# The last two output chunks of the second layer computed as seven block products

## The chip, the cores and the metric

The kernel runs on one core of a Trainium2 chip. The metric is the device time in microseconds of one execution; the median of the runs is compared.

## The reference, cut to what matters

The network is two layers of a hybrid encoder trunk (256 tokens, width 2048). Everything that the change touches is the last line of a layer:

```
merged = jnp.zeros_like(x)
for n, (y, z) in enumerate(((y_a, a_z), (y_b, b_z), (y_c, c_z), (y_m, m_z))):
    branch = y.reshape(B, S, W).astype(dt) * jax.nn.silu(z)
    merged = merged + jax.nn.sigmoid(gate_all[:, :, n]) * (branch @ w_branch[n])
return x + merged @ w_out
```

`merged` is 256 x 2048 and `w_out` 2048 x 2048, both float32. The output of the second layer is the result of the kernel.

## The kernel before, in words

**Matrix products.** Weights stream from DRAM in slabs of 512 rows by 512 columns (1 MB, a tile `raw`, four buffers, loaded by the SP queue). A slab is cut in two halves of 256 rows. ACT rounds a half to a float32r tile `whi`, DVE takes the difference as `wlo` (`cut_piece`, both 128x1024); four buffers each. The activations are cut in the same way (`mg0h`, `mg0l` and so on), and three matmuls (high x high, high x low, low x high) stand for one float32 product. A half of a slab feeds 12 matmuls of 512 columns: two 128-row steps of the contraction, two blocks of 128 tokens, three terms.

**The stream.** `advance`, called after each half, runs waiting tasks (`pump`) and cuts the half that is four halves ahead (`split_weights`). `gemm_plan` writes down the slabs in the order of use; `plan` is that order, `cuts` says for each half whether it comes from a slab or from a chain of sums. All engines execute their instructions in the order in which this program issues them, so the order of calls in Python is the order on each queue.

**Products already in use.** Two places of each layer (group `c`, and the gate chunks 2 and 3 of each branch, `DUO`) compute two neighbouring 512-column chunks as a 2x2 block product with seven instead of eight block multiplications (`product`, `take`, `combined`). A block is 1024 rows by 512 columns of weights, against 128 tokens by 1024: 24 matmuls, four pieces of 256 rows with 6 matmuls each. The token side needs sums of the blocks of its matrix (`s1`, `s2`, `s3`, `r4`, made by `forms` on DVE and cut by ACT and DVE). The weight side needs running sums: four tiles `sum` are loaded by SP, and after each use the next block is added to them by an accumulating DMA from the POOL queue (`add_block`).

**The end of the second layer.** For each 512-column piece d of `merged`, the last branch's `bridge` adds into `acc[d]`, and the task `merged(d)` turns it: a DVE transpose inside 32x32 squares (`mgpi`), sixteen 32 KB DMA moves (`mgp`, taken in turns by POOL and SP, placed in the program by `tick`), a rest of some ticks, then the cut into `mg..h` and `mg..l`. The pieces come in the order 0, 3, 2, 1, and `w_out`'s rows are stored in that order. Then `w_out` is applied: chunks 0 and 1 side by side, chunk 2, chunk 3, each of four slabs, 16 slabs in all. `added(c)` loads the residual (`x1`, kept in DRAM) and adds it on DVE to the product in PSUM, one 128-token half after the other, and each half is stored by SP. In the last slab of chunk 3 the matmuls are sorted so that the first token half ends early.

Of the kernel before, what the change touches and what calls it, by code (L numbers as in the profile page):

```python
# [158 lines left out]
BETWEEN_PRODUCTS = (4, 3, 4, 4, 3, 2, 3)  # L159
MOVES, STEPS, BANKS, WARM = 5, 2, 2, 7  # L160
# [125 lines left out]
def gemm_plan(wmem, win, wbr, wout):  # L286
    p, cuts, starts = [], [], {}
# [24 lines left out]
    for l in range(L):  # L312
# [18 lines left out]
        pair(SIDE_ORDER, *((wout, (l * 4 + c) * DM * 512) for c in range(2)))  # L331
        for c in range(2, 4):
            add(wout, (l * 4 + c) * DM * 512, 512)
    return p, cuts, starts
# [9 lines left out]
def trunk(ctx: ExitStack, tc: tile.TileContext, x, xt, memt, ng, qkg, hg, lbl, win, wmem, wbr, wout,  # L344
# [40 lines left out]
    plan, cuts, starts = gemm_plan(wmem, win, wbr, wout)  # L385
# [31 lines left out]
    def split_weights():  # L417
        if stream.cut in starts:
            group = starts[stream.cut]
            chains[group] = [G([128, 2, 512], "sum") for h in range(4)]  # L420
            for h in range(4):
                add_block(group, STAGES[0], h)
        group, i, h = cuts[stream.cut] or (None, None, None)
        if group and i != RING:
            cut_piece(*half(512), chains[group][h])
            if i < 4:
                add_block(group, STAGES[i + 1], h)
            elif i == 4 and group[1] != "c":
# [12 lines left out]
        if group and group[1] == "c":  # L441
# [4 lines left out]
    def add_block(group, stage, h):  # L446
        adds, rows, d = stage
        to = chains[group][h].rearrange("p k n -> p (k n)")
        block = dram(win, columns(*group)[d] + (2 * rows + h // 2) * 512 * 512 + h % 2 * 1024, 2048, 1024)
        if adds:  # L450
# [732 lines left out]
    for l in range(L):  # L1183
# [44 lines left out]

        def forms(l=l):
# [3 lines left out]
            def total(out, sign, first, second):  # L1233
                for p in range(2):
                    at, a, b = (u[p] if isinstance(u, tuple) else blocks(u[:, 4 * p:4 * p + 4, :]) for u in (out, first, second))
                    (ve.tensor_add if sign > 0 else ve.tensor_sub)(at, a, b)
                    yield

            def parts(name, out):
                hi, lo = (spool.tile([128, 8, 128], F32R, tag="s", name=name + e) for e in "hl")  # L1240
                ac.copy(hi, out)
                yield
                ve.tensor_sub(lo, out, hi.bitcast(F32))
                yield
                return hi, lo

# [155 lines left out]
        def bridge(n, d, gt, l=l):  # L1402
# [12 lines left out]
            if n == BR_ORDER[-1]:  # L1415
                mg.append(stream.add(merged(d)))

# [25 lines left out]
        nx = []  # L1443
# [19 lines left out]
        wo = [(wout, (l * 4 + c) * DM * 512) for c in range(4)]  # L1463
        gemms(mg, wo[:2], 512, ["wo", "wo"], order=[(i, b, j) for i, b in SIDE_ORDER for j in range(2)], then=[added(0), added(1)])
        later = [added(c) for c in (2, 3)]
        for c in (2, 3):
            later[c - 2](gemm(mg, *wo[c], 512, "wo", tail=l == L - 1 and c == 3))
        if l + 1 < L:
            xh, rs = nx, stream.add(scale_of(nssq, list(nx), 1))
# [50 lines left out]
```

## Time and profile before

| | us |
|---|---|
| median of 3 runs (1810.14 to 1810.40) | 1810.35 |
| the profiled execution | 1809.55 |
| its span, first to last instruction | 1807.5 |
| around the span | 2.05 |

The profile is of one execution. In its rows PE is TensorE's matmuls, PEld its weight loads, DVE VectorE, ACT ScalarE, POOL GpSimd, SP the SyncE that issues DMAs; `SPq` marks the issue of a DMA on that queue. Busy times of engines overlap, and the row of matmuls shows the modelled length of each, which is longer than the distance from one to the next. Times in a timeline are from the start of the span.

### The profile page before, as it was taken

How to read it: one execution, taken by the hardware profiler on the slowest of the kernel's cores; microseconds unless marked ns; L12 is line 12 of the kernel's file. 1: busy time of each engine (PE TensorE's matmuls, PEld its weight loads, DVE VectorE, ACT ScalarE, POOL GpSimd, SP SyncE). 2: the span in 40 equal slices, each digit the busy share in tenths (PEclk: the TensorE clock that was granted, in tenths of full speed). 3: DMA queues.
4: the chain of work that ended last, by engine and by line, in shares of the span. 5: the costliest groups of instructions: out<-in, count | busy, mean ns of one | idle time of the engine just before them, and what ended most of it. 6: DMA issues, size and time to landing. Idle time of an engine off the chain costs nothing.

```text
span 1807.5 us, 24344 instructions
## 1 busy us (share of the span) xinstructions
PE 1801.9 (100%) x8836; PEld 1499.9 (83%) x8836; DVE 1345.9 (74%) x1458; ACT 1059.3 (59%) x1261; POOL 379.9 (21%) x573
## 2 busy tenths in 40 slices
PE   9999999999999999999999999999999999999999
PEld 8889888888888888888888988888888888888887
DVE  5677798786878777687666779878787877767764
ACT  5756565455667656554455656545666765656442
POOL 0022330033232111112032342003332211110200
PEclk9999999999999999999999999999999999999999
DMA  9769965779899999986694996568999989998773
GB/s 337 268 213 290 290 210 179 256 227 276 271 263 272 294 227 275 263 245 216 229 296 160 314 266 210 195 235 240 264 289 253 284 274 231 274 264 232 238 233 135
DMA packets 124936, 451.44 MB, mean 250 GB/s; under 512 B 23184, under 2 KB 44944, under 8 KB 92048
## 3 DMA queue, kind: packets, MB, share of 16 engines
q1 hardware_dynamic: 89840, 357.45, 56.7%
q0 software_dynamic: 34688, 92.18, 26.2%
q8 instruction: 69, 1.13, 0.3%
q14 instruction: 51, 0.42, 0.1%
q10 hardware_dynamic: 288, 0.26, 0.0%
HBM read 419.66 MB, written 6.29 MB: 236 GB/s over the span
## 4 chain that ended last, share of the span: by engine, by line
PE 99%; DMA 0%; DVE 0%; SPq 0%; ACT 0%; issue 0%
PE u L145 51%; PE px L145 21%; PE bw L145 10%; PE wo L145 10%; PE mv L145 2%; PE mk L145 2%; PE ixrp L145 0%; PE mov L145 0%; PE mlg L145 0%; PE bo L145 0%; PE co L145 0%; PE aov L145 0%; PE cl L145 0%; PE bs L145 0%; PE alg L145 0%; DMA raw<-in_wmem 0%
## 5 line engine op out<-in xcount | busy, mean ns | idle before, releaser
L127 DVE TENSOR_TENSOR wlo<-raw,whi 128x1024 fp32r<-128x1024 f32 (+3 forms) x556 | 655.3, 1187 | 341.0 <-ACT whi L127 335.1
L127 ACT CAST whi<-raw 128x1024 fp32r<-128x1024 f32 (+3 forms) x556 | 568.1, 1025 | 571.5 <-PE u L145 340.4
L127 DVE TENSOR_TENSOR wlo<-sum,whi 128x1024 fp32r<-128x1024 f32 x240 | 288.2, 1221 | 62.4 <-ACT whi L127 54.9
L127 ACT CAST whi<-sum 128x1024 fp32r<-128x1024 f32 x240 | 250.5, 1052 | 99.7 <-PE px L145 51.3
L127 POOL DMA_DIRECT2D sum<-in_win x152 | 137.4, 910 | 607.0 <-DVE wlo L127 556.2
L145 PE MATMUL u<-whi,x01h 128*128 128x512 f32 (+2 forms) x176 | 67.5, 383 | 0.0
L145 PE MATMUL u<-whi,x11h 128*128 128x512 f32 (+2 forms) x176 | 67.5, 383 | 0.0
L145 PE MATMUL u<-whi,x12h 128*128 128x512 f32 (+2 forms) x176 | 67.4, 383 | 0.0
L145 PE MATMUL u<-whi,x02h 128*128 128x512 f32 (+2 forms) x176 | 67.4, 383 | 0.0
L145 PE MATMUL u<-whi,x10h 128*128 128x512 f32 (+2 forms) x176 | 67.3, 383 | 0.0
L145 PE MATMUL u<-whi,x00h 128*128 128x512 f32 (+2 forms) x176 | 67.3, 383 | 0.0
L145 PE MATMUL u<-whi,x03h 128*128 128x512 f32 (+2 forms) x176 | 67.1, 381 | 0.0
L145 PE MATMUL u<-whi,x13h 128*128 128x512 f32 (+2 forms) x176 | 67.1, 381 | 0.0
L145 PE MATMUL u<-wlo,x11h 128*128 128x512 f32 (+2 forms) x176 | 67.0, 381 | 0.0
L145 PE MATMUL u<-wlo,x01h 128*128 128x512 f32 (+2 forms) x176 | 67.0, 381 | 0.0
L145 PE MATMUL u<-wlo,x12h 128*128 128x512 f32 (+2 forms) x176 | 67.0, 381 | 0.0
L145 PE MATMUL u<-wlo,x02h 128*128 128x512 f32 (+2 forms) x176 | 67.0, 381 | 0.0
L145 PE MATMUL u<-wlo,x10h 128*128 128x512 f32 (+2 forms) x176 | 67.0, 381 | 0.0
L145 PE MATMUL u<-wlo,x00h 128*128 128x512 f32 (+2 forms) x176 | 67.0, 381 | 0.0
L145 PE MATMUL u<-whi,x00l 128*128 128x512 f32 (+2 forms) x176 | 67.0, 381 | 0.0
L145 PE MATMUL u<-whi,x10l 128*128 128x512 f32 (+2 forms) x176 | 67.0, 381 | 0.0
L145 PE MATMUL u<-wlo,x03h 128*128 128x512 f32 (+2 forms) x176 | 67.0, 381 | 0.0
(496 smaller groups left out, 4488.7 us busy)
## 6 DMA issues: line engine op xcount, KB each, us to landing
raw<-in_win SPq DMA_DIRECT2D x180, 1024.0 KB, 6.5
sum<-in_win POOLq DMA_DIRECT2D x152, 512.0 KB, 8.5
sum<-in_win SPq DMA_DIRECT2D x80, 512.0 KB, 6.9
raw<-in_wbr SPq DMA_DIRECT2D x32, 1024.0 KB, 6.3
raw<-in_wout SPq DMA_DIRECT2D x32, 1024.0 KB, 5.6
raw<-in_wmem SPq DMA_DIRECT2D x12, 1024.0 KB, 6.0
raw<-in_win SPq DMA_DIRECT2D x8, 656.0 KB, 4.1
xc<-in_x SPq DMA_DIRECT2D x8, 512.0 KB, 7.1
```

The lines of the kernel that those rows point to most:

```text
L127: return call(*args, **kw)
L145: return self.engine.matmul(out, w, x, **kw)
```

## The change

Layer 1 keeps its output projection. In layer 2 the chunks 0 and 1 stay slabs of 512 rows, and the chunks 2 and 3 become seven block products, written in between by `LAST_ORDER` (pairs are chunk and slab, single numbers are products). There are two chains of sums: `sumy` (products 2, 3, 4, 6) and `sumx` (product 1); products 0 and 5 take raw slabs. `LAST_BEGIN` says how many cuts ahead a chain is loaded and added to. The token-side sums come from the turned `merged` pieces by a task `last_forms`; the last piece is turned by moves on POOL alone, and its first two task steps are made at once. The residual of chunk 0 and of chunk 3 is added by an accumulating DMA instead of DVE.

```
+LAST_ORDER = ((0, 0), (1, 0), (0, 1), (1, 1), 2, (0, 2), 1, (1, 2), 3, (0, 3), 4, 0, (1, 3), 5, 6)
+LAST_RAW, LAST_NEXT = {0: (1, 1), 5: (1, 0)}, {2: (True, 0, 1), 3: (True, 1, 1), 4: (True, 1, 0)}
+LAST_BEGIN = {2: ((AHEAD, "y", (False, 0, 0)),), 1: ((2 * AHEAD, "x", (False, 0, 1)), (AHEAD, "x", (True, 1, 1)))}
...
+    def last_product(l, i, part):
+        if i in LAST_RAW:
+            rows, d = LAST_RAW[i]
+            p.append((wout, (l * 4 + 2 + d) * DM * 512 + (2 * rows + part) * 512 * 512, 512))
+        if not part:
+            for ahead, chain, stage in LAST_BEGIN.get(i, ()):
+                begins[len(cuts) - ahead] = chain, stage
+        cuts.extend(("last", i, 2 * part + k) for k in range(2))
...
+        if stream.cut in begins:
+            chain, stage = begins[stream.cut]
+            if chain not in chains:
+                chains[chain] = [G([128, 2, 512], "sum" + chain) for h in range(4)]
+            for h in range(4):
+                last_block(chain, stage, h)
         group, i, h = cuts[stream.cut] or (None, None, None)
-        if group and i != RING:
+        if group == "last" and i not in LAST_RAW:
+            chain = "x" if i == 1 else "y"
+            cut_piece(*half(512), chains[chain][h])
+            if i in LAST_NEXT:
+                last_block(chain, LAST_NEXT[i], h)
+            return
...
+    def last_block(chain, stage, h):
+        adds, rows, d = stage
+        to = chains[chain][h].rearrange("p k n -> p (k n)")
+        block = dram(wout, ((L - 1) * 4 + 2 + d) * DM * 512 + (2 * rows + h // 2) * 512 * 512 + h % 2 * 1024, 2048, 1024)
         if adds:
             po.dma_start(to, block, accum_op=OP.add)
         else:
             sy.dma_start(to, block)
...
-        def merged(d):
-            u = yield from transposed(acc[d], "mgp", 3 if d == MERGED[-1] else 4)
-            return split(u, gen, "g", f"mg{d}")
+        def merged(d, l=l):
+            u = yield from transposed(acc[d], "mgp", *((3, (po,) if l + 1 == L else (po, sy)) if d == MERGED[-1] else (4,)))
+            if l + 1 < L:
+                return split(u, gen, "g", f"mg{d}")
+            last_rows[MERGED.index(d)] = u
+            return split(u, xtp, "xt", f"mg{d}")
+
+        def last_forms():
...
+            r4 = G([128, 8, 128], "r4")
+            yield from total(r4, -1, quarter(0, 0), quarter(0, 1))
+            last_made["s3"] = yield from parts("s3", r4)
+            while len(last_rows) < 4:
+                yield BLOCKED
+            s1, s2 = (G([128, 8, 128], name) for name in ("s1", "s2"))
+            yield from total(s1, -1, quarter(0, 1), quarter(2, 1))
+            last_made["s1"] = yield from parts("s1", s1)
+            yield from total(s2, -1, s1, quarter(0, 0))
+            last_made["s2"] = yield from parts("s2", s2)
+            yield from total(r4, 1, s2, quarter(2, 0))
+            last_made["r4"] = yield from parts("r4", r4)
...
             if n == BR_ORDER[-1]:
                 mg.append(stream.add(merged(d)))
+                if d == MERGED[-1] and l + 1 == L:
+                    mg[-1].step()
+                    mg[-1].step()
...
+    def second_column():
+        qs, us = got["qs"], got["us"]
+        ve.tensor_tensor(qs, qs, us[:, 0:1, :].to_broadcast([128, 2, 512]), op=OP.subtract)
+        yield
+        ve.tensor_tensor(us, qs, us[:, 1:2, :].to_broadcast([128, 2, 512]), op=OP.add)
+        po.dma_start(us, x1[:, :, 3 * 512:4 * 512], accum_op=OP.add)
+        yield
+        ve.tensor_sub(got["xc"][:, 1, :], got["xc"][:, 1, :], qs[:, 1, :])
+        got["less"] = True
+        yield from stream.rest(5)
+        sy.dma_start(out[:, :, 3 * 512:4 * 512], us)
...
+    def first_column(t, to):
+        xc = got["xc"]
+        ve.tensor_add(xc[:, t, :], to, xc[:, t, :])
+        sy.dma_start(out[:, t, 2 * 512:3 * 512], xc[:, t, :])
...
+    for at in LAST_ORDER:
+        if isinstance(at, tuple):
+            c, b = at
+            open_chunks[c] = gemms(mg, wo[c:c + 1], 512, ["wo"], order=[(0, b, j) for j in range(2)], tiles=open_chunks.get(c))
+            if b == 2 and c:
+                ends[c] = added(c)
+            elif b == 3:
+                (ends[c] if c else first_chunk)(open_chunks[c][0])
+        else:
+            last_take(at, 0)
+            last_take(at, 1)
```

**Place one: the last moves of `merged`.** On POOL, at the start of the output projection, the order of before and of the change; `mgp` are the moves of the turned pieces (8 for each of the first three, the rest for the last piece, d = 1), `sumx` and `sumy` adds of 512 KB, `xc` and `us` the residuals of chunks 0 and 3:

```order
 L127 DMA sum<-in_win 128x1024 x32
-L127 DMA mgp<-mgpi 32x2x128 x32
-L1514 UNCONDITIONAL_BRANCH
-L1514 ISA
+L127 DMA mgp<-mgpi 32x2x128 x28
+L127 DMA sumx<-in_wout 128x1024 x4
+L127 DMA mgp<-mgpi 32x2x128 x12
+L127 DMA sumy<-in_wout 128x1024 x12
+L127 DMA xc<-x_92 128x2x512
+L127 DMA us<-x_92 128x2x512
```

Four adds now stand between the fourth and the fifth of the sixteen moves of the last piece. On ACT, from the cut of the second piece (`mg3h`) on:

```order
 L127 CAST mg3h<-mgp 128x1024
-L127 CAST whi<-raw 128x1024 x5
+L127 CAST whi<-raw 128x1024 x3
+L127 CAST s3h<-r_14522 128x1024
+L127 CAST whi<-sumy 128x1024 x2
 L127 CAST mg2h<-mgp 128x1024
-L127 CAST whi<-raw 128x1024 x5
 L127 CAST mg1h<-mgp 128x1024
-L127 CAST whi<-raw 128x1024 x18
-L1514 UNCONDITIONAL_BRANCH
+L127 CAST whi<-sumy 128x1024 x2
```

The cut of the last piece, `mg1h`, had five slab halves between itself and `mg2h`; now it follows `mg2h` directly, ahead of the third and fourth piece of product 2 (the second pair of `whi<-sumy`).

**Place two: the token sum of product 0.** `r4` is the token side of product 0. On ACT and on DVE, from the cuts of product 4's last pieces on (`xc<-wo` copies chunk 0 out of PSUM):

```order
+L127 CAST whi<-sumy 128x1024 x2
+L127 COPY xc<-wo 128x512 x2
+L127 CAST whi<-raw 128x1024
+L127 CAST r4h<-r_14522 128x1024
+L127 CAST whi<-raw 128x1024 x7
```

```order
+L127 TENSOR_TENSOR wlo<-sumy,whi 128x1024
+L127 TENSOR_TENSOR wlo<-raw,whi 128x1024 x3
+L127 TENSOR_TENSOR r4l<-r_14522,r4h 128x1024
+L127 TENSOR_TENSOR wlo<-raw,whi 128x1024
+L127 TENSOR_TENSOR us<-us,px 128x512
```

The low part `r4l` stands behind the third of product 0's four weight pieces on DVE.

**Place three: the end.** On DVE, before and now (`xc<-px` is the first result column's add, `us` chunk 3):

```order
-L127 TENSOR_TENSOR xc<-wo,xc 128x512 x2
-L127 TENSOR_TENSOR wlo<-raw,whi 128x1024 x4
-L127 TENSOR_TENSOR xc<-wo,xc 128x512
-L127 TENSOR_TENSOR xc<-wo_14892,xc 128x512
-L1514 UNCONDITIONAL_BRANCH
+L127 TENSOR_TENSOR wlo<-sumy,whi 128x1024 x4
+L127 TENSOR_TENSOR xc<-px,xc 128x512
+L127 TENSOR_TENSOR us<-qs,us 128x1024
+L127 TENSOR_TENSOR xc<-xc,qs 128x512
+L127 TENSOR_TENSOR xc<-px,xc 128x512
```

The sum that finishes chunk 3 (`us<-qs,us`) now comes behind all four pieces of product 6 and behind the add that waits for product 5; POOL's add of the residual and SP's store of chunk 3 follow it.

## Rows read from the trace of the kernel before

**Rows 1.** The page, busy time by engine, and the chain that ended last by engine:

```profile
PE 1801.9 (100%) x8836; PEld 1499.9 (83%) x8836; DVE 1345.9 (74%) x1458; ACT 1059.3 (59%) x1261; POOL 379.9 (21%) x573
PE 99%; DMA 0%; DVE 0%; SPq 0%; ACT 0%; issue 0%
```

**Rows 2.** All waits of PE in the whole span: who waited for whom, us in total, times, longest:

```profile
PE heat L145 <- DVE warm L127: 1.1, 1, 1.1
PE mk L145 <- DVE wlo L127: 0.2, 1, 0.2
```

**Rows 3.** The chain that ended last, from 1716 us to the end: start, us, what:

```profile
1716.25 87.05 PE wo L145 x384
1803.30 0.02 issue
1803.32 0.69 DVE xc L127
```

**Rows 4.** The same chain in the stage of the gate products, one slab (`u`) and one product (`px`):

```profile
1541.95 5.44 PE u L145 x24
1547.39 5.44 PE px L145 x24
```

**Rows 5.** The timeline of DVE at the start of the output projection: start, us, engine, line, operation, count, idle time before it and who ended it:

```profile
1717.37 1.23 DVE L127 TENSOR_TENSOR wlo<-raw,whi 128x1024 fp32r<-128x1024 f32 x1 [1.49 <-ACT whi L127]
1718.51 1.22 DVE L127 TENSOR_TENSOR gate<-bw,gate 128x1024 f32<-128x1024 f32 x1
1719.77 1.22 DVE L127 TENSOR_TENSOR acc<-acc,gate 128x1024 f32<-128x1024 f32 x1
1720.91 1.22 DVE L127 TENSOR_TENSOR mg3l<-mgp,mg3h 128x1024 fp32r<-128x1024 f32 x1
...
1723.18 1.24 DVE L127 STREAM_TRANSPOSE mgpi<-acc 128x1024 f32<-128x1024 f32 x1
```

**Rows 6.** The timeline of ACT, the cut of the last piece between two halves of slabs, and a pair of copies out of PSUM:

```profile
1711.80 1.26 ACT L127 ACTIVATE gate<-u,rs1r 128x512 f32<-128x512 f32 x2
...
1743.48 1.05 ACT L127 CAST whi<-raw 128x1024 fp32r<-128x1024 f32 x1 [1.67 <-PE wo L145]
1744.44 1.05 ACT L127 CAST mg1h<-mgp 128x1024 fp32r<-128x1024 f32 x1
```

**Rows 7.** The timeline of POOL, the last piece's moves before the change, as the POOL queue issued them:

```profile
1724.71 1.58 POOL L127 DMA_DIRECT2D mgp<-mgpi  x3 [13.74 <-DVE mgpi L127]
1726.56 2.63 POOL L127 DMA_DIRECT2D mgp<-mgpi  x5 [0.27 <-issue]
```

**Rows 8.** The timeline of POOL in an earlier stage, four adds and then eight moves (`bnpt`) on the same queue:

```profile
1381.29 0.91 POOL L127 DMA_DIRECT2D sum<-in_win  x1 [5.71 <-DVE wlo L127]
1382.43 0.86 POOL L127 DMA_DIRECT2D sum<-in_win  x1 [0.23 <-issue]
1387.48 0.85 POOL L127 DMA_DIRECT2D sum<-in_win  x1 [4.19 <-DVE wlo L127]
1390.30 0.86 POOL L127 DMA_DIRECT2D sum<-in_win  x1 [1.97 <-DVE wlo L127]
1390.83 3.03 POOL L127 DMA_DIRECT2D bnpt<-bnpti  x5
1395.87 0.54 POOL L127 DMA_DIRECT2D bnpt<-bnpti  x1 [2.00 <-DMA sum<-in_win]
1398.20 0.53 POOL L127 DMA_DIRECT2D bnpt<-bnpti  x1 [1.79 <-DMA sum<-in_win]
1401.15 0.53 POOL L127 DMA_DIRECT2D bnpt<-bnpti  x1 [2.41 <-DMA sum<-in_win]
```

**Rows 9.** From issue to landing, the 28 adds of POOL from 1490 to 1700 us, then the 64 moves `mgp` of layer 2 (the row of POOL's 32 and the landing of all), then the 8 stores of the result: length of the issue min/median/max in ns, first and last start:

```profile
L127 POOL DMA_DIRECT2D sum<-in_win x28: 853/862/973, 1492.7 to 1641.9; - x28
DMA to landing us min/median/max: 5.9/8.6/10.8
...
L127 POOL DMA_DIRECT2D mgp<-mgpi x32: 533/533/587, 1685.9 to 1728.7; - x32
DMA to landing us min/median/max: 1.8/4.9/6.7
...
L1456 SPq DMA_DIRECT2D out<-xc x8: 332/338/344, 1757.3 to 1804.0; - x8
DMA to landing us min/median/max: 2.0/4.1/8.5
```

**Rows 10.** DMA from 1560 to 1640 us (80 us of the gate products): packets, MB and share of 16 engines by queue (q0 is POOL's, q1 SP's):

```profile
q0 software_dynamic: 1963, 7.18, 52.0%
q1 hardware_dynamic: 2259, 12.94, 43.7%
```

**Rows 11.** Stretches: length, busy time of PE, PEld, DVE, ACT, POOL (and instructions), granted clock, share of the 16 DMA engines, GB/s:

```profile
1738.00:1760.00 22.00, 22.00 (x99) 18.22 (x98) 12.14 (x11) 9.58 (x10) 0.00 (x0) 1.00 0.59 192
1760.00:1781.00 21.00, 21.00 (x94) 17.38 (x94) 10.84 (x10) 8.24 (x8) 0.00 (x0) 1.00 0.81 276
1781.00:1803.30 22.30, 22.29 (x99) 18.12 (x97) 8.17 (x9) 5.28 (x5) 0.00 (x0) 1.00 0.07 25
1560.00:1640.00 80.00, 80.00 (x354) 66.10 (x353) 58.04 (x50) 47.68 (x51) 12.13 (x14) 1.00 0.96 252
```

**Rows 12.** The timeline of SP, the first load of `w_out`, loads while the last piece is turned, and the last stores (four merged, the last at 1804.0):

```profile
1691.42 0.33 SPq L400 DMA_DIRECT2D raw<-in_wout  x1
...
1718.62 0.33 SPq L400 DMA_DIRECT2D raw<-in_wout  x1
...
1725.55 4.29 SPq L400 DMA_DIRECT2D raw<-in_wout  x2
...
1784.51 19.87 SPq L1456 DMA_DIRECT2D out<-xc  x4
```

**Rows 13.** The timeline of PE in the first microseconds of the span:

```profile
1.13 3.35 PE L145 MATMUL heat<-warm 128*128 128x128 f32 x14 [1.13 <-DVE warm L127]
...
5.92 0.41 PE L145 MATMUL mk<-wlo,memh 128*128 128x256 f32 x1
6.13 0.32 PE L145 MATMUL mk<-whi,meml 128*128 128x256 f32 x1
6.29 0.28 PE L145 MATMUL mk<-whi,memh 128*128 128x256 f32 x1
6.40 0.28 PE L145 MATMUL mk<-wlo,memh 128*128 128x256 f32 x1
```

More of the change, by code (lines that the diff above doesn't have):

```diff
@@ L286, in gemm_plan @@
 def gemm_plan(wmem, win, wbr, wout):
-    p, cuts, starts = [], [], {}
+    p, cuts, starts, begins = [], [], {}, {}
     def slab(*entry):
@@ L330, in gemm_plan @@
                 slab(wbr, ((l * 4 + n) * 4 + at[0]) * W * 512, 512)
[L331 to L334, printed above, removed]
+        if l + 1 < L:
+            pair(SIDE_ORDER, *((wout, (l * 4 + c) * DM * 512) for c in range(2)))
+            for c in range(2, 4):
+                add(wout, (l * 4 + c) * DM * 512, 512)
+            continue
+        for at in LAST_ORDER:
+            if isinstance(at, tuple):
+                slab(wout, (l * 4 + at[0]) * DM * 512 + at[1] * 512 * 512, 512)
+            else:
+                last_product(l, at, 0)
+                last_product(l, at, 1)
+    return p, cuts, starts, begins
 def wait_for(box, key):
@@ L384, in trunk @@
     x1 = kept.tile([128, 2, DM], F32, name="x1")
-    plan, cuts, starts = gemm_plan(wmem, win, wbr, wout)
+    plan, cuts, starts, begins = gemm_plan(wmem, win, wbr, wout)
     stream, chains = Stream(account), {}
@@ L440, in split_weights @@
         cut_piece(hi, lo, piece)
-        if group and group[1] == "c":
+        if group and group != "last" and group[1] == "c":
             ve.tensor_add(chains[group][h], chains[group][h], piece)
@@ L1227, in scaled, with total, parts @@
             return take
+        def total(out, sign, first, second):
+            for p in range(2):
+                at, a, b = (u[p] if isinstance(u, tuple) else blocks(u[:, 4 * p:4 * p + 4, :]) for u in (out, first, second))
+                (ve.tensor_add if sign > 0 else ve.tensor_sub)(at, a, b)
+                yield
+        def parts(name, out):
+            hi, lo = (spool.tile([128, 8, 128], F32R, tag="s", name=name + e) for e in "hl")
+            ac.copy(hi, out)
+            yield
+            ve.tensor_sub(lo, out, hi.bitcast(F32))
+            yield
+            return hi, lo
         def forms(l=l):
@@ L1466, in trunk, with last_plain, form @@
         for c in (2, 3):
-            later[c - 2](gemm(mg, *wo[c], 512, "wo", tail=l == L - 1 and c == 3))
-        if l + 1 < L:
-            xh, rs = nx, stream.add(scale_of(nssq, list(nx), 1))
+            later[c - 2](gemm(mg, *wo[c], 512, "wo"))
+        xh, rs = nx, stream.add(scale_of(nssq, list(nx), 1))
+    last_ready = stream.add(last_forms())
+    open_chunks, ends, got = {}, {}, {}
+    def last_plain(b, t):
+        def form(k):
+            at = b + k // 4
+            if isinstance(mg[at], Task):
+                mg[at] = stream.finish(mg[at])
+            return [u[:, k % 4, 128 * t:128 * t + 128] for u in mg[at]]
+        return form
@@ new lines, in first_chunk, with stored @@
+    def first_chunk(ps):
+        u = G([128, 2, 512], "xc")
+        for t in range(2):
+            ac.copy(u[:, t, :], ps[:, t, :])
+        po.dma_start(u, x1[:, :, :512], accum_op=OP.add)
+        def stored():
+            yield from stream.rest(5)
+            sy.dma_start(out[:, :, :512], u)
+        stream.add(stored())
+    def first_column(t, to):
+        xc = got["xc"]
+        ve.tensor_add(xc[:, t, :], to, xc[:, t, :])
+        sy.dma_start(out[:, t, 2 * 512:3 * 512], xc[:, t, :])
@@ new lines, in last_take @@
+    def last_take(i, part):
+        if not got:
+            stream.claim()
+            stream.claim()
+            got["px"] = [PB("px").rearrange("p (t n) -> p t n", t=2) for _ in range(2)]
+        name = {0: "r4", 1: "s3", 3: "s1", 4: "s2"}.get(i)
+        if name and name not in last_made:
+            stream.until(last_ready, lambda: name in last_made)
+        ps, t = {0: (0, 1), 1: (0, 1), 2: (0, 0), 3: (1, 0), 4: (1, 1), 5: (0, 0), 6: (1, 0)}[i]
+        to = got["px"][ps][:, t, :]
+        if i == 6 and "less" not in got:
+            stream.until(got["second"], lambda: "less" in got)
+        form = last_summed(name) if name else last_plain(*{2: (0, 0), 5: (2, 0), 6: (2, 1)}[i])
+        product(to, form, part, i != 5, i in LAST_RAW)
+        if not part:
+            return
+        if i == 2:
+            got["us"] = G([128, 2, 512], "us")
+            ac.copy(got["us"][:, 0, :], to)
+        elif i == 1:
+            got["qs"] = G([128, 2, 512], "qs")
+            ac.activation(got["qs"][:, 1, :], to, AF.Copy, scale=-1.0)
+        elif i == 3:
+            ac.copy(got["us"][:, 1, :], to)
+            got["xc"] = residual(2)
+        elif i == 4:
+            ve.tensor_add(got["us"][:, 0, :], got["us"][:, 0, :], to)
+        elif i == 0:
+            ac.copy(got["qs"][:, 0, :], to)
+            got["second"] = stream.add(second_column())
+        else:
+            first_column(i - 5, to)
@@ new lines, in trunk @@
+    for at in LAST_ORDER:
+        if isinstance(at, tuple):
+            c, b = at
[4 more added lines that the diff above has]
+                (ends[c] if c else first_chunk)(open_chunks[c][0])
+        else:
+            last_take(at, 0)
+            last_take(at, 1)
+    for t in list(stream.tasks):
+        stream.finish(t)
```

31 lines of the change are left out of this document (19 added, 12 removed).

## The prediction

> **What bounds the kernel now.** I read the page first: PE is busy for the whole span, and the chain that ended last is PE for 99% of it [rows 1]. The list of PE's waits then shows how full that is: two waits in 1807 us, both in the first microseconds [rows 2]. So every cut weight, every turned activation and every transfer arrives in time today, and time is the number of matmuls. The output projection of the second layer shows the rate: 384 matmuls of 512 columns in 87.05 us, 0.2267 us each, and then 4.2 us from the last matmul to the end of the span, an add of 0.69 and a store [rows 3]. A slab and a product both take 5.44 us for 24 matmuls [rows 4].
>
> Two things follow. Fewer matmuls save their 0.2267 us each; and since nothing waits today, every wait that the change makes is added in full. I walked the new order on each queue against these durations, looking for instructions that can't be ready when PE wants them. There are two such places, and a longer end.
>
> **The saving.** Chunks 2 and 3 took 8 slabs, 192 matmuls; seven products are 168. 24 x 0.2267 = **-5.4 us**.
>
> **Place one: the last piece of `merged`.** Before, the last piece's transpose started at 1723.18; moved ahead of `mg3l` and one `wlo`, it starts behind `acc<-acc,gate`, at 1720.9, and ends at 1722.3 [rows 5]. POOL issued its first move 0.3 after the transpose had ended, each taking 0.53 [rows 7, 9]: four moves, 1722.6 to 1724.7. Then come the four adds of `sumx`, 0.86 each, issued by 1728.2. Then twelve moves. An earlier queue of four adds and eight moves shows what they do [rows 8]: the first five moves go out in a row, and the sixth, seventh and eighth each start only when an add has landed, 13.4, 10.7 and 10.9 us after the adds of 1382.43, 1387.48 and 1390.30 had started, that is, always the one that stands eight places ahead. Here the eighth place behind the fourth add is the twelfth move of sixteen. So the last five moves wait until the add issued at 1727.3 has landed.
>
> When is that? By the median of single adds, 8.6 [rows 9], 1735.9; this is the lower bound, as those came in ones and twos. Upper bound: an add of 0.52 MB holds the 16 DMA engines for 3.0 us (7.18 MB in 52.0% of 80 us) and a 1 MB slab for 2.8 (12.94 MB in 43.7%) [rows 10]; four adds are 12, the two slabs that SP loads from 1725.55 on [rows 12] 5.7, and the fastest move needs 1.8 [rows 9]: 1724.7 + 1.8 + 12 + 5.7 = 1744.2. The earlier queue is nearest (four adds, then moves, beside loads [rows 8]): 1727.3 + 13.4 = 1740.7; I take 1741. The last of the five moves starts 2.1 later and lands after 1.8 to 4.9 [rows 9], 3 say: the piece is there at 1746 (1739.8 to 1751.2).
>
> Who waits: ACT's cut `mg1h`, and behind it the cuts of product 2's third and fourth piece; on DVE `mg1l` and the `wlo` of these pieces. Without a wait PE starts product 2 after four slabs, 1716.25 + 21.76, and its third piece 2.72 later, at 1740.7. With the piece landed at L, ACT cuts `mg1h` and the third `whi` (0.96 apart, 1.05 long [rows 6]), DVE `mg1l` and the third `wlo` (1.14 apart, 1.22 long [rows 5]), so `wlo` is there at L + 3.5, wanted by the second matmul at 1741.0; the fourth piece then waits 0.4 for DVE's half of `s1`. The wait is L - 1737: **+9 us** (2.8 to 14.2). Nothing covers it: PE has only the pieces that are queued behind it.
>
> The clock after such a gap: this trace has no gap in the middle, only the start of the program, where 128x256 matmuls stand 0.21 apart until 6.13, five microseconds after PE's first work, and 0.11 to 0.12 apart afterwards [rows 13]. So after a gap of 9 us the array may run at half speed for up to 5 us: 0 to +2.5, I take **+1.5 us**. [...]
>
> **Place two: product 0.** Call X the end of slab (0,3). The fourth `whi` of product 4 is cut then at the earliest, since its buffer is the one that the slab's second half used. Behind it on ACT stand two copies out of PSUM (1.26 for a pair [rows 6]), and four cuts at 0.96: `whi`, `r4h`, `whi`, `whi`. The third `whi` of product 0 is ready at X + 6.1, its `wlo` at X + 7.3, and `r4l`, next on DVE, at X + 8.5. PE ends product 4 at X + 5.44 and wants `r4l` for its third matmul, at X + 5.9: a wait of 2.6. The fourth piece's add may come late on top: product 3's fourth piece is cut by 2.4 us after product 3 began, the add issues at 2.7 and lands at 11.3 to 13.5 (8.6 to 10.8 [rows 9]), where X is 10.9; that shifts ACT's row by 0.4 to 2.6. Together 3.0 to 5.2; with fewer loads beside it than there, **+3.5 us**.
>
> **Place three: the end.** Let F be the end of product 5; PE ends 5.44 later. Product 6's fourth `whi` needs the buffer that product 5's last piece frees at F; its `wlo` ends at F + 2.4, the add of column 2's first half at F + 3.0, `us<-qs,us` at F + 4.2 (0.69, 1.22 [rows 3, 5]). POOL issues the residual's add at F + 4.5; nothing else moves then (at the end the DMA share was 0.07 [rows 11]), so it lands near the minimum, 5.9 [rows 9], at F + 10.4. SP then stores 512 KB. The last store before, 256 KB, was issued at 1804.0 [rows 12] and the span ended 3.5 later, at 1807.5; for twice the size 4.2 to 5, I take 4.6. The end is F + 15.1, that is 9.6 after the last matmul instead of 4.2: **+5.4 us**. Bounds: a landing as fast as the stores' median, 4.1, and a store of 3.5, +2.5; the median 8.6 and 5, +8.5.
>
> **Costs of nothing.** The other sums of tokens (`s3`, `s1`, `s2`: eight halves and cuts) lie beside slabs, where ACT and DVE are busy for 9.6 and 12.1 of 22 us [rows 11]; were that cover gone, each DVE half costs 0.6. The start of `sumx` and `sumy` stands between SP's moves of the first pieces and holds these up by a few us; those are wanted in the four slabs, whose cuts are ready 8 us ahead. `sumy`'s second and fourth use have 16 us between them, twice an add's landing.
>
> **Sum.** -5.4 + 9 + 1.5 + 3.5 + 5.4 = +14.0 on the profiled 1809.55: 1823.6. The median of the runs is 0.8 above the profiled execution: **1824 us**.
>
> **The rivals.**
> - *Early moves.* The last piece lands before 1737 and place one costs nothing: -5.4 + 3.5 + 5.4 = +3.5, 1814. For it: with free engines the adds need less. Against: four at 3.0 alone are over at 1738.5.
> - *Cheap adds, not slower.* One mechanism: an add holds the engines no longer than a plain load of its size (1.4 by q1's rate [rows 10]). Then four land by 1724.7 + 1.8 + 5.6 = 1732.1, the moves by 1736 and place one is free; at the end the residual lands in 3.2 instead of 5.9, +2.7; at product 0 no add is late, 2.6. -5.4 + 2.6 + 2.7 = -0.1, 1810. It decides at 1.6 us an add. Against: q0 took twice q1's time for a byte [rows 10].
> - *The DMA engines become the bound.* From the first load of `w_out` at 1691.4 to product 6, some 107 us [rows 10]: 12 slabs 34, 8 loads of chains 11.4, 16 adds 48, residuals 9, moves 6: 108 us of all engines. Then product 3 or 4 waits for its adds too, as long again as place two at its upper end, about +6: 1830. Against: the gate stage runs at a share of 0.96 without one wait [rows 2, 11], and PE's own waits give the engines time.
>
> **How the numbers follow.** My forecast 0.60, early moves 0.14, cheap adds 0.11, the DMA bound 0.15. 0.2% (3.6 us) is about what a measurement of this kernel can tell from no change. Faster than 1806.7 needs cheap adds and a shorter wait at product 0: 0.05. Within 3.6 us: the rest of cheap adds and half of early moves: 0.13. Slower: 0.82. The range, 1812.5 to 1833, goes from early moves to the DMA bound with an upper term more, and leaves out cheap adds and the far sums of all upper bounds; the forecast alone spans 1816 to 1831.
>
> **What would show it.** One gap of PE of about 9 us inside product 2, ended by ACT's `whi` or DVE's `wlo`, with `mg1h` cast right before; POOL's last five moves of `mgp` starting only after the adds landed; a granted clock below 1.0 behind the gap; a gap of 3 to 4 us at product 0 before the matmuls with `r4l`; the last matmul 9 to 10 us ahead of the end. If PE shows no gap in product 2, or if the adds land in half the time, the prediction is wrong.

## The result, and the profile after

| | before | changed |
|---|---|---|
| median, us (4 runs each) | 1810.38 | 1836.34 |
| the profiled execution | 1809.55 | 1835.12 |
| its span | 1807.5 | 1833.3 |
| from the last matmul to the end of the span | 4.2 | 10.2 |

The change makes the kernel slower: ratio 1.0145, 95% interval 1.0133 to 1.0157, 26 us on the medians and 25.6 between the two profiled executions. Predicted were 1824 us (1812.5 to 1833): the right sign, 12 us too little, and the time lies above the range.

The page of the changed kernel, matmuls (busy time, share, count) and the chain that ended last; before, [rows 1], PE was 99% of that chain and nothing else counted:

```profile
PE 1801.6 (98%) x8812; PEld 1497.3 (82%) x8812; DVE 1369.4 (75%) x1482; ACT 1077.8 (59%) x1283; POOL 400.6 (22%) x599
PE 94%; DMA 4%; DVE 0%; ACT 0%; issue 0%; SPq 0%; POOL 0%; ACTq 0%; POOLq 0%
```

The three largest of PE's waits from 1716 us on (who waited for whom, us in total, times, longest), where before there was none [rows 2]:

```profile
PE px L145 <- ACT whi L127: 14.3, 2, 13.0
PE px L145 <- DVE r4l L127: 3.7, 1, 3.7
PE px L145 <- DVE wlo L127: 1.4, 2, 0.8
```

The stretches of [rows 11] in the changed kernel, and the one ahead of them: length, busy PE, PEld, DVE, ACT, POOL, granted clock, share of the DMA engines, GB/s:

```profile
1716.25:1738.00 21.75, 21.75 (x97) 18.02 (x96) 16.41 (x15) 10.05 (x10) 8.99 (x14) 1.00 1.01 286
1738.00:1760.00 22.00, 8.31 (x26) 6.07 (x25) 7.25 (x8) 6.07 (x7) 6.79 (x10) 0.69 0.80 194
1760.00:1781.00 21.00, 21.00 (x93) 17.30 (x93) 16.33 (x16) 14.26 (x15) 3.46 (x4) 1.00 0.76 197
1781.00:1803.30 22.30, 16.41 (x62) 12.16 (x61) 14.18 (x15) 11.43 (x13) 4.54 (x5) 0.93 1.06 258
```

Two stretches lose time, and in both the granted clock is below 1.00 as well. The DMA engines, whose share was 0.59, 0.81 and 0.07 in the last three of these stretches before [rows 11], are full ahead of the first gap (1.01) and all through the stretch of the second (1.06).

**The first gap.** The timeline of PE: the last matmul of product 2's second piece, the gap, and the restart (start, length, idle time before it and who ended it):

```profile
1740.29 0.39 PE L145 MATMUL px<-whi,mg0l 128*128 128x512 f32 x1
1753.71 0.79 PE L145 MATMUL px<-whi,mg3h 128*128 128x512 f32 x1 [13.04 <-ACT whi L127]
1755.16 0.80 PE L145 MATMUL px<-wlo,mg3h 128*128 128x512 f32 x1 [0.66 <-DVE wlo L127]
1755.75 0.63 PE L145 MATMUL px<-whi,mg3l 128*128 128x512 f32 x1
1756.18 0.63 PE L145 MATMUL px<-whi,mg3h 128*128 128x512 f32 x1
```

Matmuls that start 0.23 apart before the gap start 0.43 apart behind it. Product 2 began at 1737.80 and the slab behind it at 1759.61: 21.8 us for 24 matmuls that take 5.44 [rows 4], so 16.4 are lost, of them 2.0 to the clock (the last 11 matmuls took 4.45 instead of 2.49).

What ended it, on POOL (`mgp` are the last piece's moves) and on ACT:

```profile
1724.91 3.62 POOL L127 DMA_DIRECT2D sumx<-in_wout  x4
1728.33 2.94 POOL L127 DMA_DIRECT2D mgp<-mgpi  x5
1736.84 0.53 POOL L127 DMA_DIRECT2D mgp<-mgpi  x1 [5.58 <-DMA sumx<-in_wout]
1741.84 0.53 POOL L127 DMA_DIRECT2D mgp<-mgpi  x1 [4.47 <-DMA sumx<-in_wout]
1747.13 0.53 POOL L127 DMA_DIRECT2D mgp<-mgpi  x1 [4.76 <-DMA sumx<-in_wout]
1747.99 2.24 POOL L127 DMA_DIRECT2D mgp<-mgpi  x4 [0.32 <-DMA mgp<-mgpi]
...
1751.67 1.04 ACT L127 CAST mg1h<-mgp 128x1024 fp32r<-128x1024 f32 x1 [17.07 <-DMA mgp<-mgpi]
```

The last five moves do stand behind the fourth add, as in [rows 8], but that add landed at 1747.1, 20.2 us after its issue, where [rows 9] had 10.8 as the longest. The landing of the four adds (shortest, median, longest):

```profile
DMA to landing us min/median/max: 5.5/13.3/20.2
```

The first landed after 5.5 us, at 1730.4; the moves show the others at 1736.8, 1741.8 and 1747.1: one every 5.0 to 6.4 us.

The late issue of those last moves is the smaller part of it. The five moves ahead of them were issued from 1728.33 on without a wait, and they came no earlier. The chain that ended last shows the first of the five (start, us, what):

```profile
1728.33 19.38 DMA mgp<-mgpi
```

It landed at 1747.71, 0.6 us after the fourth add; the other four took 17.8 to 19.0 us. So moves that were handed over behind the adds on POOL's queue landed behind them, waited for or not. The last move was issued at 1749.69 and landed at 1751.45, which leaves at most 3.7 us to the wait for the issue.

**The second gap and the end.** The chain that ended last, behind 1778 us (start, us, what):

```profile
1778.85 12.47 DMA sumy<-in_wout
...
1798.58 1.23 DVE r4l L127
...
1799.85 6.90 PE px L145 x22
...
1812.19 10.89 PE px L145 x48
```

Product 4 began at 1786.94 and slab (1,3), two products on, at 1806.59: 19.65 instead of 10.88, 8.8 lost. An add for product 4's last piece landed after 12.47 us and delayed product 0 to 1795.38, by 3.0; the third matmul with `r4l` starts at 1799.85 instead of 1795.83, 4.0; and the 22 matmuls from there to 1806.59 take 6.74 instead of 4.99, 1.75 of clock.

At the end the store of chunk 3 waits for the residual's add (the timelines of POOL and SP):

```profile
1822.33 1.08 POOL L127 DMA_DIRECT2D us<-x  x1 [26.23 <-DVE us L127]
...
1828.90 0.60 SPq L1566 DMA_DIRECT2D out<-us  x1
```

The sum of what is lost and won: -5.4 + 16.4 + 8.8 + 6.0 = 25.8, which is the difference of the two spans (1833.3 and 1807.5); the profiled executions differ by 25.6. So no other loss of any size is in it.

### The profile page after: what moved, and what is told of

Its sections match the earlier page's. It is cut to its first block, busy times and chain, and to the rows that moved or that the text cites. A ratio compares the mean times of both kernels' runs of the same rounds, so it can differ in the third digit from the quotient of the medians.

```text
span 1833.3 us, 24392 instructions
## 1 busy us (share of the span) xinstructions
PE 1801.6 (98%) x8812; PEld 1497.3 (82%) x8812; DVE 1369.4 (75%) x1482; ACT 1077.8 (59%) x1283; POOL 400.6 (22%) x599
## 4 chain that ended last, share of the span: by engine, by line
PE 94%; DMA 4%; DVE 0%; ACT 0%; issue 0%; SPq 0%; POOL 0%; ACTq 0%; POOLq 0%
PE u L145 50%; PE px L145 22%; PE bw L145 9%; PE wo L145 6%; PE mv L145 2%; PE mk L145 2%; DMA sumy<-in_wout 1%; DMA mgp<-mgpi 1%; DMA raw<-in_wout 1%; PE ixrp L145 0%; PE mov L145 0%; PE mlg L145 0%; PE co L145 0%; PE bo L145 0%; PE aov L145 0%
## 5 line engine op out<-in xcount | busy, mean ns | idle before, releaser
L127 DVE TENSOR_TENSOR wlo<-raw,whi 128x1024 fp32r<-128x1024 f32 (+3 forms) x548 | 645.2, 1186 | 314.3 <-ACT whi L127 309.3
L127 ACT CAST whi<-raw 128x1024 fp32r<-128x1024 f32 (+3 forms) x548 | 559.3, 1024 | 536.7 <-PE u L145 339.3
L127 POOL DMA_DIRECT2D mgp<-mgpi x72 | 38.4, 549 | 152.1 <-issue 94.0
```

The source lines that it names most:

```text
L127: return call(*args, **kw)
```

## The experiments

Medians are given against the kernel before on the same chip (1809.9 to 1810.4). The third leaves the adding out, and the fourth puts transfers into the kernel before; the others do the changed kernel's work in another order or on another engine.

**1. The adds behind the moves.**

```
-... 1: ((2 * AHEAD, "x", (False, 0, 1)), (AHEAD, "x", (True, 1, 1)))}
+... 1: ((2 * AHEAD, "x", (False, 0, 1)), (6, "x", (True, 1, 1)))}
```

> The four adds of sumx are put behind all sixteen moves of the last piece on POOL. Theory (the moves wait only because of the eighth-place wait on the adds): place one goes away whole, 16.4 us of gap and half clock, and the adds, now 6.4 us later, reach product 1 up to 3 us late: 1820 to 1823. Rival (the DMA engines are the bound from 1716 us on, so the bytes are late wherever they stand): the wait comes back as 6 to 12 us at product 1, 3 or 4: 1826 to 1832.

Measured 1823.1, ratio 1.0068 (1.0053 to 1.0083): 13.2 us less. The timeline of PE, all its waits behind 1738 us:

```profile
1742.16 0.50 PE L145 MATMUL px<-wlo,mg3h 128*128 128x512 f32 x1 [0.95 <-DVE wlo L127]
1778.47 0.51 PE L145 MATMUL px<-whi,s2h 128*128 128x512 f32 x1 [1.73 <-ACT whi L127]
1779.73 0.50 PE L145 MATMUL px<-wlo,s2h 128*128 128x512 f32 x1 [0.76 <-DVE wlo L127]
1785.81 0.79 PE L145 MATMUL px<-whi,r4l 128*128 128x512 f32 x1 [3.26 <-DVE r4l L127]
```

With the adds behind the moves on POOL's queue the gap of 13 us is gone. Of the 16.4 us that place one cost, product 2 still loses 1.8 (it starts at 1737.96, the slab behind it at 1745.15), and place two costs 10.0 instead of 8.8, in part because the half clock behind its gap lasts 5.2 us instead of 3.4. Whether the moves were held up by the wait for their issue or by the adds' bytes, the next run asks.

**2. The moves shared with SP.**

```
-... ((3, (po,) if l + 1 == L else (po, sy)) if d == MERGED[-1] else (4,))
+... ((3, (po, sy)) if d == MERGED[-1] else (4,))
```

> The adds stay where they are; the last piece is turned by POOL and SP in turns, as before the change. On POOL only two moves then stand eight places behind an add, the first and the second one (landed at 1736.8 and 1741.8 in the changed kernel). Theory (queue order): the piece lands some 6 us earlier, near 1745, and the time is about 1830. Rival (the moves are late because the adds fill the engines, not because they wait for their issue): SP's eight moves are as late as POOL's, the gap stays at 13 us, 1836.

Measured 1836.2: no gain, my theory's 1830 was wrong. POOL's last move now waits for the second add only, and SP issues the rest. POOL's timeline:

```profile
1737.24 0.53 POOL L127 DMA_DIRECT2D mgp<-mgpi  x1 [5.21 <-DMA sumx<-in_wout]
```

And the chain that ended last, at SP's last move:

```profile
1737.89 13.46 DMA mgp<-mgpi
```

The last of the sixteen moves is issued almost 12 us earlier than in the changed kernel (1737.9 against 1749.7), but it, 32 KB, takes 13.46 us, where the longest of these moves before was 6.7 [rows 9], and it lands at 1751.35, as late as in the changed kernel. SP's queue had bytes of its own ahead of it: a slab issued at 1730.97 took 15.7 us. On POOL's queue the four moves that were issued behind the adds without a wait took 15.9 to 16.1. So it is the bytes already handed to the engines that hold the piece up; the wait for the issue stands for the most part in their shadow. The first run escapes both, because there the moves are handed over ahead of the adds. A queue with nothing of its own ahead of the moves was not tried.

**3. Plain loads in place of the adds.**

```
-        if adds:
+        if adds and chain == "x":
+            po.dma_start(to, block)
+        elif adds:
             po.dma_start(to, block, accum_op=OP.add)
```

> The four adds of sumx are plain loads of the same 512 KB at the same place of POOL's queue (product 1 then lacks the first block of its sum). Theory (an add costs twice the engine time of a load, the rest of the delay is the slabs that share the engines): 4 x 1.3 to 1.4 us less, the piece lands at 1746, the time is about 1831. Rival (an add is held up by itself, by what it reads and writes back, and not by its share of the engines): the loads land some 10 us after their issue, the gap shrinks to 0 to 3 us, 1820 to 1823.

Measured 1831.9, 4.4 less (expected 1831). POOL's moves behind the loads:

```profile
1726.72 2.15 POOL L127 DMA_DIRECT2D sumx<-in_wout  x4
...
1737.50 0.53 POOL L127 DMA_DIRECT2D mgp<-mgpi  x1 [3.55 <-DMA sumx<-in_wout]
1741.81 0.53 POOL L127 DMA_DIRECT2D mgp<-mgpi  x1 [3.77 <-DMA sumx<-in_wout]
```

The fourth load landed 15.1 us after the first was issued; the fourth add, 22.2. An add costs 1.8 us more than a load, here, and a load is late too.

**4. The adds alone.** In the kernel before, at a point where the DMA engines are nearly idle:

```
+            for rest, accum in ((0, True), (4, False)):
...
+                    ve.memset(u, 0.0)
...
+                    if accum:
+                        po.dma_start(u, block, accum_op=OP.add)
+                    else:
+                        po.dma_start(u, block)
```

> The kernel before, with four adds of 512 KB from POOL at about 1781 us, where its DMA engines stand nearly still, and four plain loads of the same size some 13 us later, all into tiles that nothing reads. Theory (contention): alone, the adds land 2.7 to 3.0 us apart, the fourth 12 to 15 us after the first one's issue, the loads 1.4 apart, the fourth after 6 to 8. Rival (an add is slow by itself): the adds land 5 us apart, the fourth 20 us after issue, as in the changed kernel. The time stays at 1810 to 1811 by both.

The four adds' issue, in POOL's timeline:

```profile
1787.64 0.95 POOL L127 DMA_DIRECT2D probe<-in_wout  x1 [57.26 <-DVE probe L127]
1788.99 0.87 POOL L127 DMA_DIRECT2D probe<-in_wout  x1 [0.40 <-issue]
1790.02 1.74 POOL L127 DMA_DIRECT2D probe<-in_wout  x2 [0.16 <-issue]
```

From issue to landing (the last number, us) of the first, second and third, in the list of DMA issues:

```profile
probe<-in_wout POOLq DMA_DIRECT2D x1, 512.0 KB, 5.5
...
probe<-in_wout POOLq DMA_DIRECT2D x1, 512.0 KB, 7.5
...
probe<-in_wout POOLq DMA_DIRECT2D x1, 512.0 KB, 9.0
```

The fourth took 10.7. They land at 1793.1, 1796.5, 1799.0 and 1801.6: 2.5 to 3.4 apart, the fourth 14 us after the first's issue, as the theory had it. Beside SP's slabs the same four took 22.2, the difference of 8.2 is three slabs at 2.8 (by [rows 10]). The four plain loads decided nothing: their issue was 1.1 to 2.5 apart, by DVE's memsets. The time was 1812.9, not 1810 to 1811: the probe's loads ran beside the last stores, and the span ended 6.8 us after the last matmul.

**5. The end early, and the sum for product 0 early.** Two runs, one edit each:

```
-        if i == 6 and "less" not in got:
+        if i == 5 and not part:
             stream.until(got["second"], lambda: "less" in got)
```
```
+        if i == 3 and part and "r4" not in last_made:
+            stream.until(last_ready, lambda: "r4" in last_made)
```

> Nothing but the end: the sum that finishes chunk 3 and its accumulating residual are issued before product 5 instead of behind product 6's pieces. Theory (the tail of 10.2 us is the add's landing of 6.5 and a store behind it): the last matmul stands 4.2 us ahead of the end again, as before the change, and the time is 6.0 lower, 1830.3. Rival (the moved sum, 1.22 us on DVE, and the add beside the last loads hold up product 5 or 6): 1832 to 1835, with a wait of PE after 1812.

> Nothing but place two: the sum for product 0 and its cut are issued before product 4's cuts. Theory (4.0 us for the low part of r4 behind product 0's third weight piece, and 1.75 of half clock that only this gap sets off; the late add's 3.0 stay): 1836.3 - 5.75 = 1830.6. Rival (the gap is the late add's and the cut only stands in its shadow, so product 0's own pieces are late instead): 3 us or less are won, 1833 to 1836.

Measured 1832.0 for the first, 4.4 less of the 6.0 expected: the span ends 4.8 us after the last matmul instead of 10.2, and a wait of 0.80 for a `wlo` at 1820.29 is new, since DVE makes the sum ahead of product 6's pieces. Measured 1827.7 for the second, 8.6 less, more than expected, and only half of it for the expected reason. The gap for `r4l` and its half clock are gone, but place two fell from 8.8 to 4.4 (product 4 starts at 1788.23, slab (1,3) at 1803.46), by less than the 5.75 expected. The other half is the end: with the `r4` steps out of the way the task that finishes chunk 3 also ran earlier in the program, and the end shrank by 4.6 (the last add on DVE at 1820.28, the span's end at 1825.9). What is left at place two is the late add, 13.5 us from issue to landing now.

**6. The later cut.** The adds where they were, only the cut of the last piece three ticks later:

```
-... ((3, (po,) if l + 1 == L else (po, sy)) if d == MERGED[-1] else (4,))
+... (((6, (po,)) if l + 1 == L else (3, (po, sy))) if d == MERGED[-1] else (4,))
```

> The adds and the moves stay where they are; only the cut of the last piece is put three task ticks later in the program, so that on ACT it stands behind the first cut of sumx instead of ahead of product 2's third piece. Theory (the piece lands near 1751 in any case, and what the gap costs is set by what stands behind its cut on ACT): product 2 runs through, the second cut of sumx waits for it, its wlo is there at about 1756 where product 1 wants it at 1751.4, a gap of 4 to 5 us and 0 to 1.7 of half clock in place of 16.4: 1825 to 1827. Rival (all that the DMA engines bring is late by then, the slabs and sumx too): a gap of 10 us or more stays, 1831 to 1836.

Measured 1830.5, 5.8 less: the gap is what the theory said, the sum isn't. PE's timeline at product 1:

```profile
1754.18 0.80 PE L145 MATMUL px<-whi,s3h 128*128 128x512 f32 x1 [5.27 <-ACT us L127]
```

And the same product in the chain that ended last:

```profile
1754.18 8.00 PE px L145 x24
```

5.27 us of gap in place of 13.04, then product 1 in 8.00 instead of 5.44. Part of the gain is given back at products 4 and 0, which lose 12.5 us instead of 8.8. There product 0 starts 4.9 us late instead of 3.0 (the add took 13.4, and matmuls stood 0.43 apart from 1786.2 on), `r4l` costs 4.6 instead of 4.0, and the 22 matmuls behind it take 8.0 instead of 6.7.

**7. Together.** The edits of 1 and 5; then product 0 also ahead of product 4 (`..., 3, (0, 3), 0, 4, (1, 3), 5, 6`; the task that finishes chunk 3 then starts behind product 4):

> The three edits together: sumx's adds behind the last moves, the sum for product 0 early, the end early. Theory (they add up): 1823.1 - 6.0 for the end, and of the 9.4 us that place two has in the kernel with the first edit alone, all but the late add's 3: 1810.7. Rival (the DMA engines, full from 1716 us on, are the bound once the gaps are gone): the adds for products 4 and 6 come later still, 4 to 8 us more at product 4 or 6, 1815 to 1819.

> As the three edits together, and product 0 stands before product 4, so that 5.44 us more lie between product 3 and product 4 for the adds that product 4 needs. Theory (the late add is a matter of distance): its 3 us go, 1807 to 1808, the seven products win 0.1 to 0.2% over the kernel before. Rival (the engines are the bound): the adds are late wherever product 4 stands, 1811 to 1816.

Measured 1812.45, ratio 1.0015 (1.0005 to 1.0025), and 1809.03, ratio 0.9996 (0.9986 to 1.0005). Each lies between theory and rival. In the first, place two still costs 3.7, with the late add (it cost 10.0 in experiment 1, where the expectation has 9.4). With all three costs mended and the late add given more distance, the seven products are worth what they cost: no difference from the kernel before. PE's waits in the second, in its timeline:

```profile
1741.19 0.50 PE L145 MATMUL px<-whi,mg3h 128*128 128x512 f32 x1 [0.52 <-ACT whi L127]
1742.64 0.50 PE L145 MATMUL px<-wlo,mg3h 128*128 128x512 f32 x1 [0.95 <-DVE wlo L127]
...
1800.06 0.50 PE L145 MATMUL px<-wlo,mg1h 128*128 128x512 f32 x1 [0.40 <-DVE wlo L127]
```

Product 2 still loses 2.4 us at the last piece (the slab behind it starts at 1745.66, 7.9 us after the product), product 6 another 0.6, and the end is 5.0 instead of 4.2: 3.8 of the 5.4 us that the fewer matmuls save.

**8. Where the wait goes next.** Three tries to get below. First the later cut on top, and chunk 0's residual by DVE:

```
-            if b == 2 and c:
+            if b == 2:
...
-                (ends[c] if c else first_chunk)(open_chunks[c][0])
+                ends[c](open_chunks[c][0])
```

> All that has been won so far (sumx's adds behind the last moves, the sum for product 0 early, the end early, product 0 ahead of product 4), the last piece's cut three ticks later, and chunk 0's residual by DVE from a plain load instead of an accumulating DMA. Theory (what is left in the trace with the swap is 2.7 us of gap at the last piece's cut and 2 at product 6's last sum, whose adds stand behind chunk 0's residual on POOL): most of both goes, 1805 to 1807, 0.15 to 0.25% below the kernel before. Rival (the DMA engines are full up to the end and the next byte is late in place of the last one): 1808 to 1811, no difference from the kernel before.

Measured 1812.64, ratio 1.0019 (1.0010 to 1.0028): the rival's cause, and a time above its range too. The gap at the last piece is gone; eight adds then go out in a row from 1734 on, and one of them lands after 24.67 us, in the chain that ended last, which shows the slab behind product 3 too:

```profile
1740.49 24.67 DMA sumy<-in_wout
...
1770.12 7.00 PE wo L145 x24
```

PE's timeline where it is waited for:

```profile
1766.36 0.73 PE L145 MATMUL px<-whi,s1h 128*128 128x512 f32 x1 [1.96 <-ACT whi L127]
```

The short gap at product 3 is followed by a slab in 7.00 us instead of 5.44. Then sumx without any adds by DMA: product 0 ahead of product 1, DVE adds the raw pieces (the edit below), and last the same sums on GpSimd:

```
+LAST_ORDER = (..., 2, (0, 2), (1, 2), 3, (0, 3), 0, 4, 1, (1, 3), 5, 6)
...
+        if group == "last" and i == 0:
+            ve.tensor_add(chains["x"][h], chains["x"][h], piece)
...
```

> The four adds of sumx are not made by DMA at all: product 0 stands ahead of product 1, and DVE adds the raw pieces that product 0 has loaded anyway to sumx (four adds of 1.22 us on DVE in place of some 11 us of all DMA engines). Order of the products 2, 3, 0, 4, 1, 5, 6 with a slab or two between; the sum for product 0 early, the end early, the last piece's cut two ticks later. Theory (the DMA engines are the bound from 1716 to 1780 us, and every gap of the kernels so far is that backlog in another place): no gap is left there, the engines fall below full between 1738 and 1781, 1804 to 1806, 0.2 to 0.3% below the kernel before. Rival (DVE, which was busy for 17 to 19 of each 22 us, becomes the bound with 4.9 us more, or product 0 so early lacks its token sum): gaps ended by wlo or r4l, 1809 to 1814.

> As the kernel with sumx's sums on DVE, but GpSimd makes them, which has nothing else to do from 1760 to 1777 us, and the sum that finishes chunk 3 is issued right behind product 1. Theory (in that kernel each of the 0.6 us gaps of product 0 is DVE's, which alternates a wlo and a sum at 1.14 each where PE takes 1.36 for a piece; with the sums off it neither DVE nor the DMA engines are full): the gaps of product 0 and the long end go, 1805 to 1807, 0.15 to 0.3% below the kernel before. Rival (a sum on GpSimd takes several us, no row so far shows one, or it slows DVE down while it runs): product 1 waits for its pieces and the adds of product 6 stand behind the sums, 1810 to 1816.

Measured 1816.0, ratio 1.0032 (1.0022 to 1.0042), above the rival's range, and 1815.1, ratio 1.0030 (1.0018 to 1.0041), inside it. With the sums on DVE the DMA engines do fall below full (0.90 from 1760 to 1781, 0.56 behind it), and DVE is what ends every wait but one. PE's waits for it:

```profile
PE px L145 <- DVE wlo L127: 6.2, 7, 2.1
```

And the stretch in which five of the seven lie, where DVE is busy for 19.88 of 21 us:

```profile
1760.00:1781.00 21.00, 17.17 (x69) 12.35 (x68) 19.88 (x20) 14.00 (x16) 4.32 (x6) 1.00 0.90 236
```

The longest of the seven lies behind it, at 1801.07, and the end takes 7.3 us instead of 4.2. With the sums on GpSimd, the timelines of POOL and DVE, and PE's one long wait:

```profile
1758.62 9.64 POOL L127 TENSOR_TENSOR sumx<-sumx,raw 128x1024 f32<-128x1024 f32 x4
...
1758.81 10.01 DVE L127 TENSOR_TENSOR s<-s,mgp 128x512 f32<-128x512 f32 x1
...
1770.01 0.79 PE L145 MATMUL wo<-wlo,mg1h 128*128 128x512 f32 x1 [7.05 <-DVE wlo L127]
```

A sum of 0.68 us on DVE, issued 0.2 us behind GpSimd's first, took 10.01: it stood until GpSimd's fourth was done.

## Why the prediction was wrong, and what of it was right

The forecast added up to a loss of 14.0 us, the measured sum is 25.8. Nearly all of the difference lies in place one (10.5 with its clock, measured 16.4) and in place two (3.5, measured 8.8). In both the step that failed is the date at which an accumulating DMA lands.

**The saving, -5.4.** Right: 24 matmuls fewer, and the undisturbed slabs and products still take 5.44 to 5.47.

**Place one, +9 and +1.5 for the clock; measured 14.4 and 2.0.** The order is as predicted: the four moves, the four adds, the last five moves issued behind the fourth add, one gap inside product 2 ended by ACT's `whi`, with `mg1h` right before. The step that failed is the one that dates the fourth add's landing. It took the earlier queue [rows 8] for the nearest case and 1741 for the landing, and for the upper bound, 1744.2, it counted the two slabs that SP issues from 1725.55 on. Both are too early: 1747.1. From 1724 to 1752 the two queues took of the engines (packets, MB, share):

```profile
q0 software_dynamic: 1096, 2.66, 48.9%
q1 hardware_dynamic: 897, 3.71, 35.7%
```

SP's queue held 35.7% of 28 us, 10.0 us, where the bound allowed 5.7: a slab issued at 1720.28 had not landed, SP's own moves of the piece before came on top, and the loads of [rows 12] that the bound took for two slabs were three in the changed kernel, issued at 1725.46, 1727.70 and 1731.17. A count of slabs from a date on was the wrong measure. As long as SP's queue had a slab, each add took an add's time and a slab's, 5.0 to 6.4 us, where it takes 2.5 to 3.4 alone (experiment 4). The three slabs landed at 1737.4, 1742.3 and 1747.5, each 0.4 to 0.6 us behind an add. An add's 2.5 to 3.4 and a slab's 2.8 [rows 10] make 5.3 to 6.2, close to those distances; how the engines share the two queues the trace does not show.

The prediction also gave the smaller part of the reason: it had the last five moves wait for their issue, and gave the five ahead of them no landing. These five landed behind the adds too, 17.8 to 19.4 us after their issue, and experiment 2, which issued the last move almost 12 us earlier, gained nothing. It was right that POOL's order is what can be mended (experiment 1).

**Place two, +3.5; measured 8.8.** The cut of `r4` behind the third piece was found, and the path behind it fits: with ACT's row shifted by s, `r4l` comes 2.6 + s after PE wants it. The term that was mis-sized is s. The fourth `whi` of product 4 was cut at 1791.41, 4.5 us after product 4 began at 1786.94, and not 0.4 to 2.6, as the add's landing took 12.5 us and not 8.6 to 10.8 (the engines were full there as well, a share of 1.06 where I expected fewer loads beside it). 2.6 + 4.5 is 7.1; the trace has 3.0 + 4.0. Experiment 5 bears this out: with the cut of `r4` early, 4.4 us go, the 2.6 and the clock's 1.75, and the late add's 4.4 stay. And a term was missing: a gap of 3.7 us has its half clock too, 1.75; I had given one to the long gap only.

**Place three, +5.4; measured 6.0.** Right within its bounds: the add landed in 6.6, the store took 4.4. The end made early (experiment 5) gave 4.4 of it back.

**The rivals.** Early moves and cheap adds are refuted: alone the adds land 2.5 to 3.4 us apart, where the bytes of a slab take 1.4 for 512 KB [rows 10]. The third, that the DMA engines become the bound, was given 0.15 as a case of its own; it is a part of what happened. It works inside places one and two, and in the first kernel of experiment 8 it gave a landing of 24.67 us. It is not the only reason why mending the places doesn't bring the 5.4 us: what is left in the second kernel of experiment 7 are waits for cuts by ACT and DVE of at most 0.95 us and a longer end, and the last two kernels of experiment 8 were held up by DVE. The range left it out at the upper end: all the upper bounds together reach 1835 (25.0 on 1809.55, and 0.8), and I had called that a far sum. The terms are not independent, one backlog makes both landings late.

**What is not settled.** Whether an order of slabs, products and loads exists in which the seven products win was tried in five kernels (experiments 7 and 8), the best of them equal to the kernel before; that none does is not shown. Nor was a queue tried on which nothing stands ahead of the last piece's moves, or a stream of slabs that makes room for the adds. How much of product 0's later start in experiment 6 is the clock's and how much the add's was not separated.

## What to carry to other kernels

Before work is moved from PE to DMA, sum the engine time of all queues over the stretch between the first possible issue and the use, with an accumulating DMA at its own price (here 2.5 to 3.4 us for 512 KB, about twice the 1.4 of a load's bytes [rows 10]), and take a landing beside a queue that is never empty at twice its time (here 5.0 to 6.4). A short transfer on which PE waits must be handed over ahead of the bulk ones on its queue: here 32 KB behind the adds took 17.8 to 19.4 us on POOL's queue, and 13.46 on SP's, behind slabs, and the order turned round took 13.2 us off the time (experiment 1). Where two upper bounds rest on the same backlog, the range has to take them together.

## What the runs showed of the hardware that was not expected

**The clock after short gaps.** After the gap of 3.66 us matmuls stood 0.43 apart for 3.4 us, after that of 13 for 5.4 (granted clock 0.53 and 0.50). Shorter gaps were enough elsewhere. In the first kernel of experiment 8 gaps of 1.96 and 0.53 us at product 3 were followed by 7 us of half clock (0.51 from 1766.4 to 1773.3), and in the second one gap of 2.07 us by 3.4 (0.51 from 1801.9 to 1805.3). Gaps of 1.29 and 0.75 at the end of the changed kernel's product 4 were not followed by any. Gaps of the same length came out differently: 1.68 and 0.76 us in experiment 6 were followed by half clock (0.52 from 1786.2 to 1788.7), 1.69 and 0.76 in the second run of experiment 5 were not (1.00 from 1796.2 to 1799.6). What tells gaps of one length apart no run here shows.

**GpSimd and DVE.** While GpSimd made four sums of 2.4 us in a row (9.64 us from 1758.62), one DVE operation with two operands in SBUF, 0.68 us at 1754.12 of the same run, took 10.01 us. It began 0.2 us behind the first of the four and ended 0.6 us behind the last (1768.8 against 1768.3). DVE didn't get in between the four; what held it the trace does not show.
